# Moving diagonal, level-32 and decay-copy work off VectorE in a bidirectional HGRN2 scan, with uneven filler between half heads

## The chip, the cores and the metric

The kernel runs on one core of one Trainium2 chip. The core has a matmul engine (TensorE, PE in the profile; PEld is its weight load), VectorE (DVE), ScalarE (ACT), GpSimd (POOL) and SyncE (SP), each with its own instruction queue that runs in order. Data is moved by DMA, issued here from the SP queue and from the POOL queue. The metric is the device time of one execution in microseconds. The kernel before takes 1859.93 us, the median of three runs (1857.55 to 1863.16).

## The reference

One layer of a bidirectional encoder on x of 1 x 1024 x 1024, float32. The parts that matter here are the token mixers; the convolution module and the feed-forward net stand around them.

```
h    = rmsnorm(x)
proj = h @ w_in                  # glu, q, v, z_f, z_b, og, g_a, g_b
a    = convolution module(glu)
o    = scan(q, z_f, v) + reversed scan(q, z_b, v)      # 8 heads of 128
b    = (rmsnorm of each head of o) * norm_w * silu(og)
x    = x + (sigmoid(g_a) * a + sigmoid(g_b) * (b @ o_w)) @ w_out
x    = x + conv_glu_ffn(rmsnorm(x));   out = rmsnorm(x)

# scan, per head, for one direction:
f   = lb + (1 - lb) * sigmoid(z);   k = (1 - lb) * sigmoid(-z)
S_t = diag(f_t) S_{t-1} + k_t v_t^T;   o_t = S_t^T q_t
```

Inside a chunk of 128 positions the scan becomes a matrix of scores (each pair of positions with the product of the decays between them), and from chunk to chunk a 128 x 128 state is carried, forward for one direction and backward for the other.

## The kernel before

A matmul of the large projections is done three times (high part by high part, high by low, low by high; lines 144 to 146 in `mm3`), with each operand split by ScalarE (line 122, the high part) and VectorE (line 119, the rest). The projection runs in three stretches. A first part of `w_in` runs beside the convolution module, as pairs of column tiles by a seven-product scheme; its weight sums are accumulating DMAs from the POOL queue (line 242). The last 22 column tiles of `w_in` are kept as `dense`, a stream of small steps. One step of `dense` is six matmuls of 128 x 512. They are the filler of the head stage. After the head stage come the projections `hgrn_o_w` and `w_out`, and the feed-forward net.

The head stage (lines 1123 to 1160) goes over eight heads and, inside each, two half heads of 512 positions (four chunks of 128). Everything on PE stands in the order of the program, so the loop itself sets what PE does. On the other engines a scheduler orders the instructions ahead of time, within what the data allows, and each engine's queue then runs in that order.

For each half head there are these parts:

- `scan_inputs` loads q and the two gate inputs and makes f and the keys on ScalarE; line 872 clips f on VectorE.
- `scan_base` turns f into products of decays within blocks of 8 positions, in a buffer `DE` (lines 890 to 909, VectorE), and makes the scaled queries and keys `Qh`, `Kh`, `qF` and `kG` (lines 919 to 931). It is run one half head ahead, in small steps (`ahead.step`).
- `scan_levels` builds the scores `S_t` (128 x 4 x 128) in levels of 8, 16, 32 and 64 positions. At each level ScalarE copies the keys into `A` (line 945), PE multiplies (line 948), and the result is put into the places of `S_t` that belong to the level: at 8 by a plain copy (line 972) and two predicated copies for the blocks of 8 (line 975), at 16 and 32 by a predicated copy under a mask (line 979), at 64 by two block copies on ScalarE (line 983). VectorE then scales `kG` and `qF` for the next level. The diagonal of the second direction is kept apart in one buffer `dg` (line 977), and added to `S_t` at the end (line 995, VectorE).
- `scan_states` transposes `kG`, copies it (`kT`, line 1006) and makes the state updates (line 1013).

The outputs of a head are made while the next head runs. `outputs` first carries the backward states through (line 1106, six steps on VectorE), and then `scan_outputs` multiplies (line 1054), sums squares on ScalarE (line 1059), takes the reciprocal root on POOL (lines 408 and 409, `rstd_small`), scales on ScalarE (line 1073), transposes and gates (line 1082) and stores. Its `yield`s cut it into places.

The loop calls `between` seven times per half head: four times in the levels, three in the states. Each call issues `FILL` steps of `dense` (a fraction is carried over), two steps of the base of the next half head, and one place of the pending outputs:

```
            def between(fill):
                dense.fill(fill)
                if ahead is not None:
                    ahead.step(BASE_STEPS)
                pending.fill(1)
```

After the loop the last head's outputs are issued by hand among what is left of `dense` (lines 1162 to 1176).

Of the kernel before, what the change touches and what calls it, by code (L numbers as in the profile page):

```python
# [13 lines left out]
U8 = mybir.dt.uint8  # L14
AF = mybir.ActivationFunctionType
ALU = mybir.AluOpType
AX = mybir.AxisListType

P = 128
FILL = 1.3  # L20
CONV_FILL = 1.6
NPAIRS = 17
LN_FILL = 6
# [22 lines left out]
def tile_hybrid_encoder(  # L46
# [24 lines left out]
    V, A, G, T = nc.vector, nc.scalar, nc.gpsimd, nc.tensor  # L71
# [638 lines left out]
    m_b = cp.tile([P, P], U8, name="m_b")  # L710
    m_d = cp.tile([P, P], U8, name="m_d")
    m_16 = cp.tile([P, P], U8, name="m_16")
    m_32 = cp.tile([P, P], U8, name="m_32")

    def build_masks():
        it = mp.tile([P, P], I32, tag="tm", name=nm("it"), bufs=4)
        ip = mp.tile([P, P], I32, tag="tm", name=nm("ip"), bufs=4)
        G.iota(it, pattern=[[1, P]], base=0, channel_multiplier=0)
        G.iota(ip, pattern=[[0, P]], base=0, channel_multiplier=1)
        xo = mp.tile([P, P], I32, tag="tm", name=nm("xo"), bufs=4)  # L720
        V.tensor_tensor(xo, it, ip, op=ALU.bitwise_xor)
        fs = mp.tile([P, 4, P], F32, tag="tm", name=nm("fs"), bufs=4)
        V.tensor_copy(fs[:, 0, :], xo)
        V.tensor_tensor(fs[:, 1, :], it, ip, op=ALU.subtract)
        ge = fs[:, 1, :]
        V.tensor_scalar(m_d, fs[:, 0, :], 0.0, None, op0=ALU.is_equal)
        V.tensor_scalar(fs[:, 2, :], fs[:, 0, :], 8.0, None, op0=ALU.is_lt)
        V.tensor_scalar(fs[:, 3, :], ge, 0.0, None, op0=ALU.is_ge)
        V.tensor_tensor(m_f, fs[:, 2, :], fs[:, 3, :], op=ALU.mult)
        V.tensor_scalar(fs[:, 3, :], ge, 0.0, None, op0=ALU.is_lt)  # L730
        V.tensor_tensor(m_b, fs[:, 2, :], fs[:, 3, :], op=ALU.mult)
        for m, h in ((m_16, 16.0), (m_32, 32.0)):
            V.tensor_scalar(fs[:, 2, :], fs[:, 0, :], h, None, op0=ALU.is_ge)
            V.tensor_scalar(fs[:, 3, :], fs[:, 0, :], 2 * h, None, op0=ALU.is_lt)
            V.tensor_tensor(m, fs[:, 2, :], fs[:, 3, :], op=ALU.mult)

    build_masks()

# [109 lines left out]
    def c4(t):  # L848
        return t.rearrange("p (c t) -> p c t", c=4)
# [25 lines left out]
    def scan_base(ins):  # L875


        q, f, kk, ks = ins

        def two(t, *r):  # L880
            if len(r) == 1:
                return view(t, r[0], [[8, N2]])
            return view(t, r[0], [[r[1] - r[0], 2], [8, N2]])

        fv = lambda *r: two(f, *r)
        ed = lambda *r: two(DE, *r)
        D = D0


        V.tensor_copy(ed(2, D + 4), fv(3, 4))  # L890
        tt(ed(1, D + 5), fv(2, 4), fv(3, 5))
        yield
        tt(ed(0, D + 6), fv(1, 6), ed(1, D + 5))
        tt(ed(D + 7), ed(D + 6), fv(7))
        yield
        V.reciprocal(ed(D, 7), ed(0, D + 7))
        yield

        fm = hp.tile([P, 2, NB], F32, tag="fm", name=nm("fm"), bufs=2)
        turned = view(fm, NB, [[-NB, 2], [1, NB]])  # L900
        tt(turned, view(f, 0, [[H, 2], [8, NB]]), view(DE, E0, [[H, 2], [8, NB]]))
        tb = hp.tile([P, 3, NB], F32, tag="tb", name=nm("tb"), bufs=3)
# [12 lines left out]
        along = [[8, NB], [1, 8]]  # L915
        for d in range(2):
            m0, st = ((0, 1), (7, -1))[d]
            whole = [[8, NB], [st, 8]]
            tt(view(Qh, (1 - d) * H + m0, whole), view(q, m0, whole), view(DE, D + d * H, along))
            yield  # L920
            keys(
                view(Kh, d * H + m0, whole),
                view(kk, d * H + m0, whole),
                ks[:, d : d + 1],
                view(DE, d * H, along),
            )
            yield
        both = [[H, 2], [8, NB], [1, 8]]
        tt(view(qF, 0, both), view(Qh, 0, both), view(fm, 0, [[NB, 2], [1, NB], [0, 8]]))
        yield  # L930
        tt(view(kG, 0, both), view(Kh, 0, both), view(DE, D + 7, [[H, 2], [8, NB], [0, 8]]))
        yield
        yield qF, kG, [(Qh[:, 1 - d, :], Kh[:, d, :]) for d in range(2)], tb

    def scan_levels(base, S_t, Tt):
# [28 lines left out]
        def over(m):  # L964
            return view(m, 0, [[0, 4], [1, P]])

        for h in (8, 16, 32, 64):
# [3 lines left out]
            if h == 8:  # L971
                A.copy(S_t, b)
                for d, m in ((0, m_f), (1, m_b)):
                    bi = inside(d)
                    V.copy_predicated(S_t, over(m), bi)
                    if d == 1:
                        V.copy_predicated(c4(dg), over(m_d), bi)
            elif h < 64:
                V.copy_predicated(S_t, over(m_16 if h == 16 else m_32), b)
            else:  # L980
                for s0 in range(0, P, h):
                    t0 = s0 ^ h
                    A.copy(S_t[s0 : s0 + h, :, t0 : t0 + h], b[s0 : s0 + h, :, t0 : t0 + h])
# [8 lines left out]
            tt(to, view(tb, 0, [[nb, k], [2, n]]), view(tb, 1, [[nb, k], [2, n]]))  # L992
            tb = tn
            yield
        V.tensor_tensor(S_t, S_t, c4(dg), op=ALU.add)

    def scan_states(i, kG, v, Tt, Sf, Sb):

# [37 lines left out]
    def scan_outputs(h, kept, Sf, Sb):  # L1036
# [28 lines left out]
            if half == 0:  # L1065
                yield
        rstd_small(rs, ss, DK)
        yield
        yield
        for half in range(2):  # L1070
            for c in range(4):
                sl = slice(c * P, (c + 1) * P)
# [28 lines left out]

    def outputs(h, kept, Tt, Sf, Sb):
        for c in range(5, -1, -1):
            hf, cc = c // 4, c % 4
            n1, c1 = (c + 1) // 4, (c + 1) % 4
            V.scalar_tensor_tensor(
                Sb[hf][:, cc, :],
                Sb[n1][:, c1, :],
                Tt[:, n1, 1, c1 : c1 + 1],
                Sb[hf][:, cc, :],  # L1110
                op0=ALU.mult,
                op1=ALU.add,
            )
        yield
        yield from scan_outputs(h, kept, Sf, Sb)
# [12 lines left out]
    for h in range(NH):  # L1128
# [4 lines left out]
        for half in range(2):  # L1133
# [13 lines left out]
            for n, _ in enumerate(scan_levels(base, S_t, Tt[:, half])):  # L1147
                if n == 2:
# [2 lines left out]
                        T.transpose(b[:, c * P : (c + 1) * P], vl[:, c * P : (c + 1) * P], ident)  # L1151
                    v = hp.tile([P, 4, DK], F32, tag="v", name=nm("v"), bufs=3)
                    A.copy(v.rearrange("p c e -> p (c e)"), b)
                between(FILL)
            qF, kG = base[0], base[1]
            for _ in scan_states(i, kG, v, Tt, Sf, Sb):
                between(FILL)
            kept.append((S_t, v, qF))
            cur = ahead
        pending = Stream(outputs(h, kept, Tt, Sf, Sb))  # L1160

    left = 8 * (len(rest) - 2) + 16 - dense.count
    pending.fill(1)
    dense.fill(left - 20)
    pending.fill(1)
    dense.fill(4)
    pending.fill(2)
    dense.fill(4)
    pending.fill(2)
    dense.fill(4)  # L1170
# [323 lines left out]
```

## Time and profile before

| | us |
|---|---|
| runs, median (lowest, highest) | 1859.93 (1857.55, 1863.16) |
| profiled execution, its own time | 1873.26 |
| profiled execution, span from first to last instruction | 1871.5 |
| PE busy in the span | 1788.6 |
| VectorE busy | 1275.7 |
| ScalarE busy | 796.2 |
| POOL busy | 185.8 |

A profile shows one execution. The page gives busy time of each engine, the span in 40 slices with the busy share of each in tenths, the costliest groups of instructions, and the DMA issues. Its other views answer for a stretch of time: busy time by stretch, which waits were long and who ended them, groups of instructions with their mean duration, and the single instructions in order of time. Rows name an instruction by engine, line of the kernel, operation, and its tiles as output<-input. PE's matmuls overlap, so its busy time is not a measure of how well it is used; gaps between its rows are.

### The profile page before, as it was taken

The numbers are of one execution on the slowest core, as the hardware profiler recorded it, in microseconds if no ns is written. First come the engines' busy times: TensorE is split into PE (matmuls) and PEld (weight loads), VectorE is DVE, ScalarE is ACT, GpSimd is POOL, SyncE is SP. The second block draws the span as 40 slices with busy tenths as digits, with TensorE's granted clock in tenths as the row PEclk, the third lists the DMA queues.
The fourth block names the chain that finished last, engine by engine and source line by source line (L and its number), as shares of the span: only waits on it lengthen the run. The fifth ranks groups of instructions, "written<-read, shape, count | busy, mean of one in ns | idle before, by whom it ended". The sixth has DMA issues, their size and how long they took to land.

```text
span 1871.5 us, 23768 instructions
## 1 busy us (share of the span) xinstructions
PE 1788.6 (96%) x8574; PEld 1481.4 (79%) x8574; DVE 1275.7 (68%) x1874; ACT 796.2 (43%) x1483; POOL 185.8 (10%) x197
## 2 busy tenths in 40 slices
PE   7989999999999999999989999899999999899996
PEld 6868777777778888888878787688888888788885
DVE  4599999534479999999835565666666667534445
ACT  6443333234545566556442244443444434522124
POOL 1201111213000000000000001111111111000000
PEclk9999999999999999999999999999999999999998
DMA  7658878775653333332238665676776765633134
GB/s 268 213 141 185 184 170 198 184 170 130 208 186 96 113 113 117 98 108 91 74 110 239 191 193 190 152 156 144 150 153 149 156 146 130 208 97 95 55 86 169
DMA packets 323468, 281.42 MB, mean 150 GB/s; under 512 B 14734, under 2 KB 246934, under 8 KB 323350
## 3 DMA queue, kind: packets, MB, share of 16 engines
q1 hardware_dynamic: 272886, 240.05, 41.4%
q0 software_dynamic: 50464, 39.85, 14.9%
q8 instruction: 67, 1.10, 0.3%
q14 instruction: 51, 0.42, 0.1%
HBM read 188.09 MB, written 71.83 MB: 139 GB/s over the span
## 4 chain that ended last, share of the span: by engine, by line
PE 45%; DVE 23%; DMA 18%; ACT 6%; issue 5%; POOL 1%; SPq 0%; ACTq 0%; POOLq 0%; DVEq 0%
PE mm L144 12%; PE mm L145 12%; PE mm L146 12%; DMA wr<-wr 4%; DVE wp L119 3%; DMA wr<-sw 3%; DMA sw<-in_w_in_dram 3%; DMA tm<-d_a 3%; DVE kG L840 2%; DVE acc L755 2%; PE sc L144 2%; PE sc L146 2%; PE sc L145 2%; DVE qF L840 2%; DVE DE L840 2%
## 5 line engine op out<-in xcount | busy, mean ns | idle before, releaser
L144 PE MATMUL mm<-hx,wp 128*128 128x512 f32 x1176 | 480.1, 408 | 23.8 <-DVE ev L541 6.8
L146 PE MATMUL mm<-hx,wp 128*128 128x512 f32 x1176 | 464.9, 395 | 1.9 <-DVE wp L119 1.9
L145 PE MATMUL mm<-hx,wp 128*128 128x512 f32 x1176 | 464.6, 395 | 0.5 <-DVE hx L476 0.5
L122 ACT CAST wp<-wr 128x1024 fp32r<-128x1024 f32 (+2 forms) x193 | 176.7, 915 | 344.8 <-PE mm L145 188.3
L119 DVE TENSOR_TENSOR wp<-wr,wp 128x1024 fp32r<-128x1024 f32 (+2 forms) x193 | 203.4, 1054 | 123.0 <-ACT wp L122 116.2
L144 PEld LDWEIGHTS mm<-hx,wp 128*128 128x128 f32 x1176 | 224.7, 191 | 72.9 <-DVE ev L541 9.7
L146 PEld LDWEIGHTS mm<-hx,wp 128*128 128x128 f32 x1176 | 224.1, 191 | 52.5 <-DVE wp L119 3.7
L145 PEld LDWEIGHTS mm<-hx,wp 128*128 128x128 f32 x1176 | 224.7, 191 | 43.0 <-DVE hx L476 0.8
L755 DVE SCALAR_TENSOR_TENSOR acc<-gl,v_b,acc 128x1024 f32<-128x1024 f32 x120 | 150.0, 1284 | 0.5
L1370 DVE TENSOR_TENSOR xr<-mm,xr 128x512 f32<-128x512 f32 x48 | 33.1, 690 | 80.4 <-PE mm L146 80.4
L948 PE MATMUL sc<-qF,A 128*128 128x128 f32 x512 | 69.8, 280 | 13.3 <-DVE qF L840 13.1
L948 PEld LDWEIGHTS sc<-qF,A 128*128 128x128 f32 x512 | 65.2, 195 | 20.4 <-issue 14.9
L242 POOL DMA_DIRECT2D wr<-sw x38 | 33.8, 889 | 442.8 <-DVE wp L119 153.1
L122 ACT CAST wq<-sw 128x1024 fp32r<-128x1024 f32 x39 | 41.0, 1051 | 77.1 <-PE mm L145 59.5
L945 ACT COPY A<-kG 128x512 f32<-128x512 f32 x64 | 39.6, 618 | 73.8 <-DVE kG L840 51.3
L1292 DVE SCALAR_TENSOR_TENSOR tm<-gp,v_a,tm 128x512 f32<-128x512 f32 x88 | 65.6, 746 | 3.3 <-ACT tm L1288 2.5
L144 PE MATMUL mm<-hy,wp 128*128 128x512 f32 x156 | 62.2, 399 | 3.1 <-ACT su L270 2.9
L145 PE MATMUL mm<-hy,wp 128*128 128x512 f32 x156 | 61.9, 396 | 0.7 <-DVE hy L119 0.7
L270 ACT COPY su<-mm 128x512 f32<-128x512 f32 x78 | 45.1, 578 | 39.2 <-PE mm L146 39.2
L144 PE MATMUL tr<-hx,wp 128*128 128x512 f32 x156 | 61.4, 394 | 0.0
L146 PE MATMUL mm<-hy,wp 128*128 128x512 f32 x156 | 61.1, 392 | 0.0
L144 PE MATMUL sc<-hy,wq 128*128 128x512 f32 x156 | 61.1, 392 | 0.0
(322 smaller groups left out, 3601.5 us busy)
## 6 DMA issues: line engine op xcount, KB each, us to landing
wr<-in_w_in_dram SPq DMA_DIRECT2D x53, 512.0 KB
sw<-in_ffn_w_up_dram SPq DMA_DIRECT2D x44, 256.0 KB
sw<-in_ffn_w_up_dram POOLq DMA_DIRECT2D x22, 512.0 KB, 9.2
wr<-in_ffn_w_up_dram SPq DMA_DIRECT2D x22, 512.0 KB
d_g<-ft SPq DMA_DIRECT2D x44, 256.0 KB
ev<-d_g SPq DMA_DIRECT2D x44, 256.0 KB
wr<-sw POOLq DMA_DIRECT2D x38, 256.0 KB, 3.2
wr<-wr POOLq DMA_DIRECT2D x38, 256.0 KB, 4.8
```

Of the source, the lines that this page charges most:

```text
L119: eng.tensor_tensor(lo, src, hi.bitcast(F32), op=ALU.subtract)
L122: A.copy(hi, src)
L144: T.matmul(acc, whi[:, k, :], ahi, start=first, stop=False, skip_group_check=again)
L145: T.matmul(acc, whi[:, k, :], alo, start=False, stop=False, skip_group_check=again)
L146: T.matmul(acc, wlo[:, k, :], ahi, start=False, stop=last, skip_group_check=again)
L242: G.dma_start(o, a, accum_op=ALU.add)
L270: A.copy(t, acc)
L755: V.scalar_tensor_tensor(acc, g[:, k : k + S], tap(k), acc, op0=ALU.mult, op1=ALU.add)
L840: V.tensor_tensor(o, a, b, op=op)
L945: A.copy(A_t.rearrange("p (b x e) -> p b x e", x=2, e=h), pairs(kG, h))
L948: T.matmul(b[:, c * P : (c + 1) * P].rearrange("p (b x e) -> p b x e", x=2, e=h), A_t[:, c * P : (c + 1) * P], view(qF, c * P, [[2 * h, P ...
L1292: V.scalar_tensor_tensor(c, g[:, o + k : o + k + H], vec("fdw", k * NF + j), c, op0=ALU.mult, op1=ALU.add,)
```

## The change

Five things are changed in the head stage, and one mask is no longer built.

1. The filler: `FILL` becomes 1.1 steps for each place of the first half head and 1.5 for the second.
2. The outputs take eleven places instead of eight: the chain of backward states is cut in two, and four places instead of two lie between the reciprocal root and the scaling. The calls after the loop are changed to match.
3. The diagonal is added to `S_t` by an accumulating DMA from the POOL queue instead of an addition on VectorE.
4. Level 32 is put into `S_t` by four block copies of 32 partitions on ScalarE, as level 64 is by two, instead of a predicated copy on VectorE. The mask `m_32` goes.
5. The first strided copy of `scan_base` (line 890) is on ScalarE instead of VectorE.

```diff
-FILL = 1.3
+FILL = (1.1, 1.5)
...
-    m_32 = cp.tile([P, P], U8, name="m_32")
...
-        for m, h in ((m_16, 16.0), (m_32, 32.0)):
-            V.tensor_scalar(fs[:, 2, :], fs[:, 0, :], h, None, op0=ALU.is_ge)
-            V.tensor_scalar(fs[:, 3, :], fs[:, 0, :], 2 * h, None, op0=ALU.is_lt)
-            V.tensor_tensor(m, fs[:, 2, :], fs[:, 3, :], op=ALU.mult)
+        V.tensor_scalar(fs[:, 2, :], fs[:, 0, :], 16.0, None, op0=ALU.is_ge)
+        V.tensor_scalar(fs[:, 3, :], fs[:, 0, :], 32.0, None, op0=ALU.is_lt)
+        V.tensor_tensor(m_16, fs[:, 2, :], fs[:, 3, :], op=ALU.mult)
...
-        V.tensor_copy(ed(2, D + 4), fv(3, 4))
+        A.copy(ed(2, D + 4), fv(3, 4))
...
-            elif h < 64:
-                V.copy_predicated(S_t, over(m_16 if h == 16 else m_32), b)
+            elif h == 16:
+                V.copy_predicated(S_t, over(m_16), b)
             else:
                 for s0 in range(0, P, h):
                     t0 = s0 ^ h
...
-        V.tensor_tensor(S_t, S_t, c4(dg), op=ALU.add)
+        G.dma_start(S_t.rearrange("p c t -> p (c t)"), dg, accum_op=ALU.add)
...
         rstd_small(rs, ss, DK)
-        yield
-        yield
+        for _ in range(4):
+            yield
...
     def outputs(h, kept, Tt, Sf, Sb):
         for c in range(5, -1, -1):
+            if c == 2:
+                yield
...
-                between(FILL)
+                between(FILL[half])
...
-    pending.fill(1)
+    pending.fill(2)
     dense.fill(left - 20)
     pending.fill(1)
     dense.fill(4)
-    pending.fill(2)
+    pending.fill(4)
```

More of the change, by code (lines that the diff above doesn't have):

```diff
@@ L1153, in tile_hybrid_encoder @@
                     A.copy(v.rearrange("p c e -> p (c e)"), b)
-                between(FILL)
+                between(FILL[half])
             qF, kG = base[0], base[1]
             for _ in scan_states(i, kG, v, Tt, Sf, Sb):
-                between(FILL)
+                between(FILL[half])
             kept.append((S_t, v, qF))
```

## The prediction

> **What bounds the kernel now.** I read the page first for the whole span, then busy time by stage, then the waits of the head stage, then its timeline. The stage in question is the loop over heads, from about 555 to 946 us.
>
> ```profile
> span 1871.5 us, 23768 instructions
> PE 1788.6 (96%) x8574; PEld 1481.4 (79%) x8574; DVE 1275.7 (68%) x1874; ACT 796.2 (43%) x1483; POOL 185.8 (10%) x197
> PE   7989999999999999999989999899999999899996
> DVE  4599999534479999999835565666666667534445
> ...
> 555.00:946.00 391.00, 370.95 (x2359) 327.27 (x2360) 359.37 (x666) 212.80 (x489) 13.79 (x14) 0.99 0.32 100
> 617.21:639.08 21.87, 18.70 (x119) 16.11 (x118) 17.72 (x35) 10.57 (x23) 1.33 (x1) 1.00 0.37 121
> 639.08:668.95 29.87, 29.74 (x195) 26.58 (x194) 29.80 (x57) 18.91 (x46) 0.61 (x2) 1.00 0.33 98
> ```
>
> The last three rows are busy time by stretch: length, then PE, PEld, DVE, ACT, POOL, clock, DMA share. Over the head stage PE is busy 370.95 of 391 us, so 20.05 us of PE idle time is all that any edit here can win, unless PE work goes away, and none does. DVE is busy 359.37 us, 92%; by the tenths DVE is at 9 only here and in the convolution stage. The last two rows are one half 1 and the following half 0, cut at the diagonal additions that end each. They are unequal. In half 0 (29.87 us) both PE and DVE are full. In half 1 (21.87 us) PE idles 3.17 us and DVE 4.15 us. Half 0 carries the previous head's outputs on top of the same seven shares of filler.
>
> What ends PE's idle time, by the waits of 560 to 935 us (waiter, releaser, total, times, longest), and two of these in the timeline:
>
> ```profile
> PE sc L948 <- DVE qF L840: 9.6, 9, 1.9
> PE sc L1013 <- ACT kT L1006: 5.6, 7, 1.3
> PE sc L961 <- ACT Sb L1031: 1.7, 2, 1.5
> ACT tm L1073 <- POOL ors L409: 9.2, 7, 1.6
> DVE kG L840 <- ACT A L945: 7.0, 4, 2.7
> ...
> 723.20 1.16 PE L1013 MATMUL sc<-v,kT 128*128 128x128 f32 x8 [0.77 <-ACT kT L1006]
> 736.31 1.13 PE L948 MATMUL sc<-qF,A 128*128 128x128 f32 x8 [1.94 <-DVE qF L840]
> ```
>
> More than half of PE's named waits are for DVE's qF update, the rest for ScalarE's kT and Sb copies. ScalarE in turn stands 9.2 us in seven heads waiting for POOL's rstd before it can scale the outputs (L1073), with kT and A copies queued behind; so an output step that comes too soon also costs.
>
> **The change part by part.** First the three operations taken from VectorE, and what stands for them on ScalarE (mean ns, 560 to 935 us):
>
> ```profile
> L979 DVE COPY_PREDICATED S<-m,sc 128x512 f32<-128x512 uint8 x28 | 20.4, 727 | 0.0
> L995 DVE TENSOR_TENSOR S<-S,dg 128x512 f32<-128x512 f32 x15 | 10.0, 668 | 0.2
> L890 DVE COPY DE<-f 128x256 f32<-128x256 f32 x14 | 6.0, 432 | 0.0
> ...
> L865 ACT ACTIVATE f<-zi,lbw 128x512 f32<-128x512 f32 x26 | 21.2, 815 | 0.1
> L983 ACT COPY S<-sc 64x256 f32<-64x256 f32 x30 | 10.9, 365 | 12.9 <-PE sc L948 9.6 <-DVE Kh L843 3.0
> L1033 ACT COPY Sb<-sc 128x128 f32<-128x128 f32 x7 | 1.9, 273 | 0.0
> ```
>
> VectorE loses, per half head, one of the two predicated copies (0.727), the diagonal addition (0.668) and the strided copy (0.432): 1.83 us, and 16 x 1.83 = 29.2 us over the stage. That is more than PE's 20.05 us of idle time, so PE must become the limit.
>
> ScalarE gains four copies of 32 partitions by 128 elements and one strided copy of 256 elements per half head. Its 128-element copy takes 0.273 and its 256-element one 0.365; I take 0.273 each (same elements per partition), 1.09 us, with 0.365 as the upper end, 1.46. The strided copy lies between 0.365 (256 elements, rows of 64) and 0.815 (512 elements with scale and bias); I take 0.45, near VectorE's own 0.432. That is 1.54 us per half head (1.46 to 2.28), 25 us over the stage. ScalarE goes from 212.8 to 238 us of some 377: 63%. As busy time it is covered; its cost can only be order, since ScalarE works in order and the new copies stand between A and kT copies that PE and VectorE wait for. Two couplings are new. VectorE's third DE product now waits for ScalarE's strided copy (in the built order it carries such a wait); two or more VectorE operations stand between, the f clip and a kG update among them, so I cost it at nothing, with 16 x 2.7 = 43 us as the upper end, from the longest wait of kG for an A copy above. And the level-32 copies let their bank go by ScalarE instead of VectorE, which no longer holds it behind its backlog: nothing, or a small gain.
>
> The diagonal goes to POOL's queue as an accumulating transfer of 256 KB inside SBUF. The weight sums use the same form and size (L242: durations of the issue on POOL; page 6: median us to landing):
>
> ```profile
> L242 POOL DMA_DIRECT2D wr<-sw x38: 865/887/932, 135.0 to 1574.5; - x38
> ...
> wr<-sw POOLq DMA_DIRECT2D x38, 256.0 KB, 3.2
> wr<-wr POOLq DMA_DIRECT2D x38, 256.0 KB, 4.8
> ...
> 614.81 0.37 ACT L983 COPY S<-sc 64x256 f32<-64x256 f32 x1
> 628.90 0.72 DVE L977 COPY_PREDICATED dg<-m_d,ob 128x512 f32<-128x512 uint8 x1
> 637.87 0.75 ACT L983 COPY S<-sc 64x256 f32<-64x256 f32 x2 [0.29 <-PE sc L948]
> 651.58 0.72 DVE L977 COPY_PREDICATED dg<-m_d,ob 128x512 f32<-128x512 uint8 x1
> 616.61 0.20 POOL L408 TENSOR_SCALAR ors<-oss 128x8 f32<-128x8 f32 x1 [97.01 <-ACT jk L1059]
> ```
>
> It can start when the last level-64 copy is done (615.18, 638.62) and the next write of the single dg buffer waits for it (628.90, 651.58): 13.7 and 13.0 us of room against 0.89 + 4.8 = 5.7. The matmuls that read S come later still. POOL is busy 13.79 us in the stage and takes 14 us more. The rstd pair of a head now stands in POOL's order behind the transfer of half 0, which is released at 615.18, before rstd's own 616.61; and the scaling that waits for rstd moves three places later. So I cost it at nothing.
>
> A rule speaks against this. The Trainium skill, page "SBUF — State Buffer", section on the two sides of the memory, says that VectorE and GpSimd share a port pair under an exclusive lock, so that descriptor writing and VectorE's two-port modes block each other whole. No row of this stage can show it, POOL issuing nothing there. It is priced below as a rival.
>
> Next, filler and outputs. The count of one fill step is six matmuls:
>
> ```profile
> 563.49 0.39 PE L146 MATMUL mm<-hx,wp 128*128 128x512 f32 x1
> 564.85 0.39 PE L146 MATMUL mm<-hx,wp 128*128 128x512 f32 x1
> ...
> 708.63 0.39 PE L1054 MATMUL ob<-Sb,qF 128*128 128x128 f32 x2
> 713.08 1.22 DVE L840 TENSOR_TENSOR qF<-Qh,fm 128x1024 f32<-128x1024 f32 x1
> ...
> L733 DVE TENSOR_SCALAR fs<-fs x2: 211/214/216, 133.2 to 136.0; 128x128 f32<-128x128 f32 x2
> ```
>
> Six matmuls from start to start are 564.85 - 563.49 = 1.36 us. Each half has seven places: half 0 goes from 9.1 to 7.7 steps and half 1 from 9.1 to 10.5, so 1.4 x 1.36 = 1.9 us of PE work moves from the full half into the one with 3.17 us of idle time. The total stays 18.2 per head, and what remains after the loop too. The outputs' eight places become eleven of fourteen: the Sb chain takes two, both output products go one place later, and scaling, transposes and stores of d_bm go four later, into half 1. On the SP queue those stores now stand behind the next loads instead of ahead, where their buffers allow it. The order also brings the first output product nearer to the qF write that reuses its buffer: it ends at 709.0 and the write starts at 713.08, 4.1 us of room. One place later costs a level, a v transpose and a fill step, about 3.0 us, which leaves 1.1; nothing, or 1 us of VectorE's relief in each of 7 heads. The places in the tail are filled to match (two, one, four, two, one), so nothing changes there. Three VectorE operations of the mask (0.2 us each) go, in the convolution stage: under 1 us.
>
> **The sum.** In half 0 PE's demand falls by 1.9 us, and VectorE's by 1.83, from the same 29.8 us: both come to 28.0. In half 1 PE takes 18.70 + 1.9 = 20.6 of 21.87 and VectorE 17.72 - 1.83 = 15.9, so both still fit. So a head saves about 1.85 us; with seven such half 0s and a little from the first head, 7.5 x 1.85 = 13.9 us, 14 us. PE's idle time of the stage would go from 20 to 6 us. All stages after are unchanged and hand it through. The profiled execution took 1873.26 us (span 1871.5), 13 us or 0.7% over the median of 1859.93; I take the difference over to the median: 1859.9 - 14 = 1846 us, range of this case 1840 (all 20 us gone) to 1853.
>
> **The rivals.**
> - The port lock: VectorE is held during each descriptor write. 16 x 0.887 = 14.2 us of VectorE's 29.2 come back and half of the gain goes: 14 - 7 = 7, so 1853. This is what the page named above would give at worst. For it: 16 clips and the products with two SBUF inputs run all the time. Against: VectorE then still has 15 us less than before.
> - ScalarE's round trips stay. Of the PE waits above, 7.3 us are for kT and Sb, and less filler in half 0 covers them less. If these double and only the qF part goes, 9.6 - 7.3 = 2 us remain: 1858, no measurable difference.
> - Slower: VectorE's DE product waits for the strided copy, which on ScalarE stands behind a kT copy that waits for PE. Its price is 16 times the lateness; it decides from 29.2 / 16 = 1.83 us, where it eats the relief. At the 2.7 us of the longest wait above: 16 x (2.7 - 1.83) = 14 us, 1874. For it: ScalarE does stand before such copies (kG for A, 7.0 us in four). Against: only four times in sixteen, and the outputs' bunch on ScalarE is thinned.
> - The transfer does not land in 13 us: each us over it costs up to 15. Its 5.7 us speak against it.
>
> **How the numbers follow.** Forecast 0.60, port lock 0.10, round trips 0.13, ScalarE's copy 0.14, late transfer 0.03. About 0.3%, 5.6 us, is what a measurement of this kernel can tell from no change. Faster holds the first two, 0.70; same 0.13; slower 0.17. The range reaches from 1838 (all idle time and 2 us of the convolution stage) to 1864, which takes in the round trips and the small end of ScalarE's copy and leaves out its 1874.
>
> **What would show it.** In the profile after, the head stage is some 14 us shorter and VectorE's busy share in it falls to about 87%; halves come nearer to 28 and 22 us; PE's idle time in it is near 6 us; the waits for qF and for ors are gone or small; POOL shows 16 issues of some 0.89 us with dg never a releaser. Wrong if DE on VectorE has waits on ScalarE, dg waits on a DMA, or kT and Sb waits of PE grow.

## The result, and the profile after

The changed kernel takes 1876.47 us (median of 5 runs, 1873.88 to 1879.20); the kernel before took 1861.05 us beside it (5 runs, 1857.55 to 1864.15). The ratio is 1.0082, 95% interval 1.0064 to 1.0101: 0.8% slower, some 15 us. The forecast was 1846 us, faster.

The work went where the change put it. The page of the kernel after, its span and its busy time by engine:

```profile
span 1874.7 us, 23882 instructions
PE 1786.6 (95%) x8574; PEld 1480.4 (79%) x8574; DVE 1254.3 (67%) x1823; ACT 818.4 (44%) x1563; POOL 200.1 (11%) x213
DVE  4599999534479888889735555666666667534445
```

DVE is 21.4 us less busy than before, ACT 22.2 and POOL 14.3 us more; in the head stage's slices DVE fell from 9 to 8 tenths. For the stage I use one cut for all kernels from here on: from the first to the last `v` copy of the sixteen half heads. Busy time by stretch of before, then of after (length, PE, PEld, DVE, ACT, POOL, clock, DMA share):

```profile
559.89:941.44 381.55, 364.27 (x2327) 321.44 (x2327) 351.89 (x653) 210.86 (x486) 13.79 (x14) 0.99 0.32 101
```

```profile
556.13:944.57 388.44, 364.88 (x2313) 321.85 (x2312) 334.12 (x611) 230.04 (x557) 26.75 (x29) 0.99 0.36 106
```

VectorE has 17.8 us less to do in the stage, and the stage is 6.9 us longer. PE does the same work; its idle time (length less PE) rose from 17.28 to 23.56 us. Which waits, from those of after in this stretch (waiter, releaser, total, times, longest):

```profile
DVE f L870 <- ACT f L863: 11.3, 7, 3.2
PE sc L946 <- DVE qF L838: 10.9, 12, 2.0
ACT tm L1071 <- POOL ors L409: 9.8, 7, 2.1
DVE kG L838 <- ACT A L943: 9.2, 7, 2.3
PE sc L959 <- ACT Sb L1029: 8.7, 5, 2.2
DVE DE L838 <- ACT DE L888: 5.8, 6, 1.2
PE sc L1011 <- ACT kT L1004: 1.4, 2, 1.2
```

Against before, PE's wait for qF is not shorter (9.6 there), that for kT fell from 5.6 to 1.4, and that for the Sb copy rose from 1.7 to 8.7 us. ScalarE still waits for `ors` in all seven heads. And VectorE, with 17.8 us less to do, idles almost 25 us more (54.3 against 29.7): its wait for `f` from ScalarE rose from 4.3 to 11.3 us, that for the keys in `A` from 7.0 to 9.2, and the one for ScalarE's strided copy (`DE`), 5.8 us, is new. The timeline of after, around one start of half 1, shows how the Sb wait comes about:

```profile
666.01 0.58 ACT L1004 COPY kT<-tr 128x512 f32<-128x512 f32 x1
668.38 1.83 POOL L409 TENSOR_TENSOR ors<-ors,mhalf 128x8 f32<-128x8 f32 x1
670.25 0.69 ACT L1071 ACTIVATE tm<-tm,ors 128x128 f32<-128x128 f32 x2 [1.96 <-POOL ors L409]
672.27 1.85 ACT L1071 ACTIVATE tm<-tm,ors 128x128 f32<-128x128 f32 x6
674.03 0.46 ACT L1029 COPY Sb<-sc 128x384 f32<-128x384 f32 x1
674.53 1.16 PE L959 MATMUL sc<-Qh,Kh 128*128 128x128 f32 x8 [1.85 <-ACT Sb L1029]
```

ScalarE waits 1.96 us for the root, does the scaling (L1071; a weight cast and the copy of a filler bank stand between its two groups), and only then copies Sb, which empties the bank that PE's next product (L959) needs. In the kernel before four of the eight scalings stood between the two kT copies instead (the same view, the same head):

```profile
667.29 0.59 ACT L1006 COPY kT<-tr 128x512 f32<-128x512 f32 x1
670.25 1.28 ACT L1073 ACTIVATE tm<-tm,ors 128x128 f32<-128x128 f32 x4 [1.37 <-POOL ors L409]
671.44 0.56 ACT L1006 COPY kT<-tr 128x512 f32<-128x512 f32 x1
```

By one mark the halves became more even. ScalarE's last block copy of level 64 marks the end of the scores of a half head; of before (the first and last of seven heads, end of half 1) and of after (the same two, and between them one half 0 and one half 1):

```profile
586.33 0.75 ACT L983 COPY S<-sc 64x256 f32<-64x256 f32 x2 [3.06 <-PE sc L948]
944.71 0.75 ACT L983 COPY S<-sc 64x256 f32<-64x256 f32 x2 [2.69 <-PE sc L948]
```

```profile
579.99 0.75 ACT L981 COPY S<-sc 64x256 f32<-64x256 f32 x2 [0.94 <-PE sc L946]
607.37 0.37 ACT L981 COPY S<-sc 64x256 f32<-64x256 f32 x1
632.18 0.74 ACT L981 COPY S<-sc 64x256 f32<-64x256 f32 x2 [2.85 <-PE sc L946]
946.64 0.74 ACT L981 COPY S<-sc 64x256 f32<-64x256 f32 x2
```

Over the seven heads half 0 takes 28.2 us on average before and 26.9 after, half 1 takes 23.0 and 25.5. Half 0 gave 1.3 us, half 1 took 2.5. (358.38 and 366.65 us in all.) That is where ScalarE stands, not PE; PE's own halves are shown under "The order taken apart".

The two profiles place 6.9 us of the loss. The rest of the 15 us can't be read from them, because before's profiled execution is itself 12 us above the median of its runs (its granted clock, 0.984, is the lowest that any execution of that kernel shows; others have up to 0.993). So the experiments are judged by the ratio of their medians, and the stage is used for which wait moved.

### The profile page after: what moved, and what is told of

Its sections match the earlier page's. It is cut to its first block, busy times and chain, and to the rows that moved or that the text cites. A ratio compares the mean times of both kernels' runs of the same rounds, so it can differ in the third digit from the quotient of the medians.

```text
span 1874.7 us, 23882 instructions
## 1 busy us (share of the span) xinstructions
PE 1786.6 (95%) x8574; PEld 1480.4 (79%) x8574; DVE 1254.3 (67%) x1823; ACT 818.4 (44%) x1563; POOL 200.1 (11%) x213
## 4 chain that ended last, share of the span: by engine, by line
PE 40%; DMA 6%; DVE 4%; ACT 2%; issue 1%; POOL 0%; ACTq 0%; POOLq 0%; SPq 0%; DVEq 0%
PE mm L144 10%; PE mm L145 10%; PE mm L146 10%; DMA tm<-d_a 3%; PE sc L144 2%; PE sc L146 2%; PE sc L145 2%; DMA sw<-in_ffn_w_up_dram 1%; PE tr L145 1%; PE tr L146 1%; PE tr L144 1%; DMA ev<-d_g 1%; DMA wr<-wr 1%; PE ob L1052 1%; DVE tm L1189 1%
## 5 line engine op out<-in xcount | busy, mean ns | idle before, releaser
L144 PE MATMUL tr<-hx,wp 128*128 128x512 f32 x156 | 61.2, 392 | 0.0
L144 PE MATMUL sc<-hy,wq 128*128 128x512 f32 x156 | 61.1, 392 | 0.0
L146 PE MATMUL sc<-hy,wq 128*128 128x512 f32 x156 | 61.0, 391 | 0.0
L146 PE MATMUL tr<-hx,wp 128*128 128x512 f32 x156 | 60.7, 389 | 0.0
```

Of the source, the lines that this page charges most:

```text
L144: T.matmul(acc, whi[:, k, :], ahi, start=first, stop=False, skip_group_check=again)
L146: T.matmul(acc, wlo[:, k, :], ahi, start=False, stop=last, skip_group_check=again)
```

## The experiments

All ratios are to the kernel before, run beside each. The waits are PE's, in the head stage; idle is the length less PE's busy time; a dash says that the view lists no such wait. The kT column holds the row `sc <- kT` alone: with the product in the other bank (`ob <- kT`) PE waited 3.8 us more for kT in e5_strided, 1.6 in e7_no_adds, 1.1 in e8_qf_first, 1.0 in e2_engines, and 0.6 or less elsewhere.

| run | ratio (95% interval) | stage us | PE idle | qF | kT | Sb |
|---|---|---|---|---|---|---|
| before | 1 | 381.55 | 17.28 | 9.6 | 5.6 | 1.7 |
| after | 1.0082 (1.0064, 1.0101) | 388.44 | 23.56 | 10.9 | 1.4 | 8.7 |
| e1_order | 1.0064 (1.0038, 1.0091) | 389.00 | 24.23 | 11.9 | 0.6 | 9.5 |
| e2_engines | 1.0054 (1.0033, 1.0076) | 388.00 | 22.16 | 10.4 | 5.8 | 2.0 |
| e3_diag | 1.0019 (0.9999, 1.0038) | 381.10 | 16.08 | 8.6 | 6.8 | - |
| e4_scalar | 1.0058 (1.0036, 1.0079) | 387.45 | 22.40 | 7.7 | 8.0 | 1.9 |
| e5_strided | 1.0101 (1.0082, 1.0119) | 396.20 | 26.29 | 7.0 | 5.5 | 2.5 |
| e6_level32 | 1.0043 (1.0027, 1.0059) | 383.80 | 19.42 | 6.7 | 11.5 | 0.3 |
| e7_no_adds | 0.9998 (0.9984, 1.0013) | 376.60 | 15.36 | 5.8 | 6.9 | - |
| e8_qf_first | 1.0009 (0.9994, 1.0024) | 384.50 | 16.96 | 3.5 | 8.6 | 1.8 |
| e9_places | 1.0024 (1.0008, 1.0041) | 386.71 | 19.84 | 11.3 | 0.5 | 7.2 |
| e10_fill | 0.9998 (0.9983, 1.0013) | 381.08 | 18.10 | 5.4 | 11.2 | 1.0 |
| e11_spare | 1.0031 (1.0013, 1.0048) | 387.46 | 20.63 | 8.3 | 10.0 | 1.7 |
| e12_gap6 | 0.9961 (0.9941, 0.9980) | 372.32 | 10.46 | 6.4 | 3.2 | 0.8 |
| e13_gap4 | 1.0006 (0.9982, 1.0030) | 378.33 | 14.37 | 4.1 | 6.2 | 1.6 |
| e14_cut_gap5 | 1.0005 (0.9984, 1.0026) | 384.23 | 19.34 | 10.4 | 0.9 | 6.5 |
| e15_gap6_diag | 0.9967 (0.9948, 0.9986) | 369.64 | 9.78 | 5.1 | 3.3 | - |
| e16_gap6_full | 0.9993 (0.9971, 1.0015) | 374.60 | 12.35 | 6.1 | - | 3.0 |
| e17_gap8 | 0.9968 (0.9950, 0.9986) | 372.08 | 10.66 | 6.0 | 3.3 | 1.0 |
| e18_gap6_qfirst | 0.9932 (0.9912, 0.9952) | 368.42 | 7.00 | 2.9 | 2.7 | 1.0 |

**The order or the engines?** e1_order is before with parts 1 and 2 of the change (uneven filler, eleven places), e2_engines is before with parts 3 to 5 (diagonal, level 32, strided copy).

> The uneven filler and the eleven places alone; diagonal, level 32 and strided copy stay on VectorE. Theory A (the order costs: the scaling of the outputs now stands on ScalarE at the start of half 1, ahead of the Sb copy that the second product of level 8 waits for): this alone is slower by 8 to 16 us than before, and PE's waits for Sb are as long as in the changed kernel (8.7 us against 1.7 before). Theory B (the work moved to ScalarE costs): within 4 us of before or faster by some us, because filler moved into the half with idle time. Theory C (the DMA costs): as B.

> Diagonal by DMA, level 32 and strided copy on ScalarE; filler 1.3 and eight places as before. Theory A: faster than before by 5 to 15 us, as VectorE is relieved of 29 us. Theories B and C: slower by 8 to 16 us, with VectorE's waits for ScalarE longer than before.

Both are slower than before, so neither half of the change is a gain spoiled by the other. Only e1_order has the Sb waits (9.5 us) of the changed kernel. The loss of e2_engines, 7.7 us, is just under the 8 expected. The two losses, 0.64 and 0.54%, add to more than the 0.82% of both together, but by no more than the intervals allow; whether they share idle time is open.

**The three moves one at a time.** e3_diag, e4_scalar (4 and 5 together), e5_strided, e6_level32:

```diff
-        V.tensor_tensor(S_t, S_t, c4(dg), op=ALU.add)                      # e3
+        G.dma_start(S_t.rearrange("p c t -> p (c t)"), dg, accum_op=ALU.add)
-        V.tensor_copy(ed(2, D + 4), fv(3, 4))                              # e4, e5
+        A.copy(ed(2, D + 4), fv(3, 4))
-            elif h < 64:                                                   # e4, e6
+            elif h == 16:
```

> Only the diagonal moves, to the accumulating DMA. Theory C: slower by 8 us or more, VectorE waiting for the DMA before it writes dg, or its clip and its products lengthened beside the descriptor writes. Theories A and B: faster by 2 to 8 us, as VectorE loses 10.7 us of 359 in the head stage and nothing waits.

> Only level 32 and the strided copy move, to ScalarE. Theory B: slower by 8 us or more; the strided copy, 0.7 us on ScalarE against 0.43 on VectorE, keeps VectorE's third DE product waiting, and the four copies delay kT, Sb and A copies. Theories A and C: faster by 3 to 10 us, as VectorE loses 18.5 us.

> Only the strided copy moves to ScalarE. If it is the costly one of the two of the run before (0.7 us on ScalarE in place of 0.43, in front of A and kT copies): slower by 5 us or more. If the four level-32 copies are: within 3 us.

> Only level 32 moves to ScalarE, the mask of 32 goes. If the four copies are the costly ones (about 1.05 us per half head in ScalarE's order, between the A copies): slower by 5 us or more, with PE waiting longer for kT and A copies. If the strided copy is: within 3 us or faster.

The transfer can't be told from no change; the 2 to 8 us that two of the theories gave it did not come. The loss of e2_engines is that of the two moves to ScalarE. In e6_level32 PE's kT wait doubles, 5.6 to 11.5 us. The strided copy alone is the worst kernel of all, though less is on ScalarE than in e4_scalar; so it isn't busy time that costs but what happens to stand ahead of what. One such place, from its timeline:

```profile
931.85 1.23 DVE L840 TENSOR_TENSOR qF<-Qh,fm 128x1024 f32<-128x1024 f32 x1
932.33 3.32 POOL L408 TENSOR_SCALAR ors<-oss 128x8 f32<-128x8 f32 x1 [46.69 <-ACT jk L1059]
932.99 0.69 DVE L840 TENSOR_TENSOR qF<-qF,tb 128x512 f32<-128x512 f32 x1
933.59 0.69 DVE L995 TENSOR_TENSOR S<-S,dg 128x512 f32<-128x512 f32 x1
934.19 1.23 DVE L840 TENSOR_TENSOR kG<-Kh,DE 128x1024 f32<-128x1024 f32 x1
937.40 0.40 ACT L1073 ACTIVATE tm<-tm,ors 128x128 f32<-128x128 f32 x1 [5.16 <-POOL ors L409]
937.82 0.58 ACT L1006 COPY kT<-tr 128x512 f32<-128x512 f32 x1
938.46 1.16 PE L1013 MATMUL ob<-v,kT 128*128 128x128 f32 x8 [1.75 <-ACT kT L1006]
```

POOL's first step of the root, 0.20 us in most heads, takes 3.32; ScalarE stands 5.16 us before the scaling, the kT copy behind it, and PE behind that. It happens once at this length in that execution. Of the stage's 14.65 us over before, 9.0 are PE's idle time, in the main waits for A (5.7 us, none before) and for kT (9.3 us with both products, 5.6 before); 5.6 are busy time of PE. Why this order is so much worse than e4_scalar's stays open.

**Is VectorE the bound?** e7_no_adds leaves out the level-32 write into `S_t` and the diagonal addition, and gives them to nobody (its output is not the reference's):

> Level 32 is not put into the scores at all and the diagonal is not added (its output is therefore not the reference's); the mask of 32 is not built. VectorE loses 22 us and no engine gains work. If VectorE's load bounds the head stage, as the prediction had it: faster by 8 to 15 us. If the order of the engines' round trips bounds it, and not VectorE's load: within 4 us of before, VectorE's busy share falling to about 87%, PE's idle time in the stage staying above 14 us.

No change, 0.9998, though VectorE's busy time in the stage fell by 13.7 us, to 338.23. The qF waits of that profile fell by 3.8 us and those for kT rose by 2.9 (both products), and the runs are no faster. In this order VectorE's load is not what the time goes by.

**One round trip eased.** e8_qf_first issues VectorE's qF update ahead of the writes of the scores:

```diff
             tt(pairs(kG, h), pairs(kG, h), view(tb, 1, [[2, n], [nb - 1, 2], [0, h]]))
+            tt(pairs(qF, h), pairs(qF, h), view(tb, nb + 1, [[2, n], [nb - 1, 2], [0, h]]))
...
-            tt(pairs(qF, h), pairs(qF, h), view(tb, nb + 1, [[2, n], [nb - 1, 2], [0, h]]))
```

> The kernel before, with the update of qF issued ahead of the writes into the scores at each level, so that VectorE does it earlier; no work is added or taken away. If PE's waits for qF (13 us in the stage) come from the place of that update in VectorE's order: they fall below 6 us and the kernel is faster by 3 to 8 us. If they come from VectorE's load: no change beyond 3 us.

The 13 us of the expectation are the wait for qF over the whole span; in the stage it was 9.6. The waits of e8_qf_first:

```profile
PE sc L1013 <- ACT kT L1006: 8.6, 7, 3.2
PE sc L948 <- DVE qF L840: 3.5, 3, 1.7
```

The qF wait fell by 6 us and the kT wait took 3 to 4 of it: nothing gained (1.0009).

**The order taken apart.** e9_places is part 2 alone, e10_fill part 1 alone:

> The kernel before with the eleven places of the outputs alone (the Sb chain cut in two, four places instead of two ahead of the scaling, the calls after the loop to match); the filler stays at 1.3 for each place, VectorE and ScalarE keep their work. If the loss of the order (1.0064 for uneven filler and eleven places together) comes from where the scaling stands on ScalarE: PE's waits for the Sb copy at about 9 us as there, those for kT near 1.5 us, ratio 1.004 to 1.008. If it comes from the uneven filler: waits for Sb near 2 us and a ratio within 0.3 % of 1. By the prediction (the outputs' bunch on ScalarE is thinned): qF and ors waits gone, faster by 5 to 14 us.

> The kernel before with the uneven filler alone (1.1 steps for each place of the first half head, 1.5 for the second), the outputs in eight places. By the prediction: 1.9 us of PE work for each head goes from the full half into the idle time of the other, faster by up to 14 us, 0.993. If round trips bound and the filler between is what covers them: half 0, where the outputs already cover, loses little and half 1 gains little, ratio 0.998 to 1.002, PE idle of the stage near the 17 us of before. If the uneven filler is what costs in the order: 1.004 to 1.008.

The filler is neutral. It trades qF waits (9.6 to 5.4) for kT waits (5.6 to 11.2): in the stage, of before and of e10_fill alike, every wait for kT stands in half 0, which loses filler, and all but one of those for qF in half 1, which gains it. The eleven places cost 0.24%, less than the 0.4% or more that the theory gave, and bring the Sb waits.

What each half gained or lost has to be read on PE itself. PE runs in program order, so its first product inside the blocks of 8 (`sc<-Qh,Kh`) cuts the halves where the program does. The means of the profiled executions from one such row to the next, over half 0 of the last seven heads and half 1 of heads two to seven:

| us | half 0 | PE busy | idle | half 1 | PE busy | idle |
|---|---|---|---|---|---|---|
| before | 27.8 | 26.7 | 1.1 | 23.6 | 22.2 | 1.4 |
| e10_fill | 26.7 | 24.9 | 1.8 | 24.7 | 23.9 | 0.8 |
| e9_places | 28.0 | 26.3 | 1.7 | 24.1 | 22.9 | 1.1 |
| after | 27.3 | 24.5 | 2.8 | 25.5 | 25.0 | 0.5 |

In e10_fill the 1.9 us of filler did move, but half 0 became only 1.1 us shorter, since PE waits longer for kT in it, and half 1 became as much longer. In the changed kernel half 0 has 2.2 us less of PE's work and is 0.5 us shorter: PE idles 2.8 us in it, of which the waits for Sb, which all stand at its end, are 1.2 (8.7 us in seven heads). By ScalarE's copies of level 64 e9_places has two equal halves, 25.9 and 25.9; PE's halves moved there by 0.5 us at most. The filler and the eleven places together cost 0.64% (e1_order); the intervals of e1_order and e9_places overlap, so whether the filler makes the places worse is open.

**ScalarE's time by itself.** e11_spare adds the level-32 copies and lets VectorE keep its own:

```diff
                 V.copy_predicated(S_t, over(m_16 if h == 16 else m_32), b)
+                if h == 32:
+                    spare = hp.tile([P, 4, 32], F32, tag="spare", name=nm("spare"), bufs=2)
+                    for s0 in range(0, P, h):
+                        t0 = s0 ^ h
+                        A.copy(spare[s0 : s0 + h, :, :], b[s0 : s0 + h, :, t0 : t0 + h])
```

> The kernel before with the four 32-partition level-32 copies on ScalarE done in addition, into a spare tile; VectorE keeps its predicated copy, so ScalarE takes 16 x 4 x 0.256 = 16.4 us more and VectorE nothing less. If what costs is ScalarE's time ahead of its A and kT copies: slower by at least as much as with the copies moved (1.0043), kT and A waits of PE above 8 us. If the cost there came from the order that the move gave to VectorE or from the bank being held by ScalarE: at or below 1.002.

Slower by 0.31%, with kT waits of 10 us. e6_level32 with VectorE relieved is 0.43% slower (the intervals overlap): no gain from the relief shows, and the copies on ScalarE cost about the same with it and without.

**Where the scaling stands.** e12_gap6 leaves the chain of backward states in one place and puts six places, not two, ahead of the scaling; e13_gap4 has four; e14_cut_gap5 has the chain cut in two and five, so that its scaling is issued at the places nine and ten, as in e12_gap6. (The changed kernel: cut, four, places eight and nine.)

```diff
         rstd_small(rs, ss, DK)
-        yield
-        yield
+        for _ in range(6):         # e13: 4; e14: 5, with the chain cut
+            yield
...
-    pending.fill(2)
+    pending.fill(6)
```

> The kernel before with six places between the reciprocal root and the scaling (two before, four in the changed kernel), so that the scaling is issued at the places nine and ten of fourteen, away from the first products of half 1; filler 1.3 everywhere, Sb chain in one place. If a scaling next to a copy that PE waits for is what costs, and its place alone decides: both waits small (kT under 3 us, Sb under 3 us), stage shorter by 3 to 6 us, ratio 0.996 to 0.999. If the round trips simply hand the wait on to the next one, as with the qF update issued first: the sum of PE's waits stays at 15 to 18 us and the ratio within 0.3 % of 1.

> The kernel before with four places instead of two between the reciprocal root and the scaling, the Sb chain in one place: the step in the placing of the outputs that the changed kernel shares with the faster kernel of six places. With the cut of the chain it gave 1.0024 and Sb waits of 7.2 us. If the cut costs (it makes both output products, the squares and the root one place later, so that ScalarE meets the root's wait in half 1's start): 0.996 to 0.999, Sb waits under 3 us. If the place of the scaling costs: 1.001 to 1.004, Sb waits of 5 us or more.

> The kernel before with the chain cut in two and five places ahead of the scaling, so that the scaling is at places nine and ten as in the faster kernel of six places, one place later than in the changed kernel; filler 1.3. If the cut costs: 1.001 to 1.004 as with the eleven places, Sb waits near 7 us. If the place of the scaling alone decides: 0.995 to 0.998, PE's named waits near 10 us as there.

e12_gap6 is faster than before. With the scaling at the same places, the cut costs 0.44% (0.9961 against 1.0005, intervals apart), and the two kernels with the cut and the even filler show Sb waits of 6.5 and 7.2 us; of those that change only places and filler, none without the cut has over 1.7. Without the cut, two places later for the scaling gain 0.45% (1.0006 to 0.9961, intervals just apart) and halve the kT waits; the first two places later, from before to e13_gap4, gained nothing (1.0006). How the cut works can be seen in the timelines around a start of half 1, first of e9_places (cut):

```profile
669.76 0.58 ACT L1006 COPY kT<-tr 128x512 f32<-128x512 f32 x1
671.54 0.43 POOL L408 TENSOR_SCALAR ors<-oss 128x8 f32<-128x8 f32 x1 [49.83 <-ACT jk L1059]
673.72 1.28 ACT L1073 ACTIVATE tm<-tm,ors 128x128 f32<-128x128 f32 x4 [0.84 <-POOL ors L409]
675.41 1.27 ACT L1073 ACTIVATE tm<-tm,ors 128x128 f32<-128x128 f32 x4
676.59 0.46 ACT L1031 COPY Sb<-sc 128x384 f32<-128x384 f32 x1
677.10 1.16 PE L961 MATMUL sc<-Qh,Kh 128*128 128x128 f32 x8 [1.93 <-ACT Sb L1031]
```

and of e12_gap6 (no cut):

```profile
660.41 0.20 POOL L408 TENSOR_SCALAR ors<-oss 128x8 f32<-128x8 f32 x1 [46.96 <-ACT jk L1059]
661.45 0.57 ACT L1006 COPY kT<-tr 128x512 f32<-128x512 f32 x1
662.41 0.70 ACT L1073 ACTIVATE tm<-tm,ors 128x128 f32<-128x128 f32 x2 [0.39 <-POOL ors L409]
664.95 1.86 ACT L1073 ACTIVATE tm<-tm,ors 128x128 f32<-128x128 f32 x6
666.71 0.46 ACT L1031 COPY Sb<-sc 128x384 f32<-128x384 f32 x1
667.23 1.16 PE L961 MATMUL sc<-Qh,Kh 128*128 128x128 f32 x8 [0.57 <-ACT Sb L1031]
```

With the cut the output products, their squares and so the root come one place later: POOL starts it 1.8 us after the second kT copy instead of 1.0 before it, and the scaling falls on the seam of the halves, where PE needs kT, Sb and A from ScalarE within a few us. A program place is not a place in ScalarE's queue, though: in e12_gap6 the scheduler still sets six scalings ahead of Sb, and what seems to help is that they are ready earlier against it (0.57 us of wait instead of 1.93). The cut also moves the output products and splits the chain on VectorE; no run separates these from the later root.

**The moves again, in the better order.** e15_gap6_diag is e12_gap6 with the transfer; e16_gap6_full is the changed kernel without the cut and with six places; e17_gap8 is e12_gap6 with eight places; e18_gap6_qfirst is e12_gap6 with the qF update first.

> The kernel before with six places ahead of the scaling and the diagonal by the accumulating transfer; VectorE loses 16 x 0.668 = 10.7 us and ScalarE takes nothing. If with the round trips eased VectorE's qF update is the wait that is left (6.4 us there): 2 to 5 us faster than with six places alone, 0.993 to 0.995. If VectorE's load is no bound here either, as in the run that left work out: 0.995 to 0.997, the same as six places alone.

> The changed kernel with the chain of backward states in one place and six places ahead of the scaling: the uneven filler and all three moves off VectorE are in it. If the loss of 0.8 % was the cut and the place of the scaling alone: 0.992 to 0.996. If ScalarE's 5 added copies per half head cost by themselves what they cost in the old order (1.0054): 1.000 to 1.003, about 0.5 % above six places alone, with waits for kT, Sb and A above 8 us together.

> The kernel before with eight places ahead of the scaling, which is then issued at the places eleven and twelve of fourteen, in the levels of half 1 and two places further from its first products than with six. If what gains is that the scaling leaves the round trips at the seam of the halves: the same as six places or better, 0.993 to 0.997. If the scaling only has to find another place, and in the levels stands ahead of A copies: A waits appear, 0.998 to 1.002.

> The kernel before with six places ahead of the scaling and the qF update issued ahead of the write of the scores. Alone, the qF update first handed its wait to kT (qF 9.6 to 3.5 us, kT 5.7 to 8.6) and gained nothing, 1.0009. If with kT and Sb eased nothing stands behind to take the wait: qF waits fall from 6.4 us to under 3, others stay under 5 us, 0.992 to 0.995. If a chain of round trips sets the pace whatever its first link: the sum of named waits stays near 10 us and the ratio at 0.995 to 0.998.

The busy time of the stage of e16_gap6_full, then of e18_gap6_qfirst with two of its waits:

```profile
559.84:934.44 374.60, 362.25 (x2313) 319.99 (x2312) 332.76 (x611) 231.64 (x557) 26.79 (x29) 1.00 0.38 110
```

```profile
555.80:924.22 368.42, 361.42 (x2319) 320.42 (x2319) 349.74 (x652) 209.65 (x485) 14.26 (x14) 1.00 0.32 101
PE sc L948 <- DVE qF L840: 2.9, 5, 1.1
PE sc L1013 <- ACT kT L1006: 2.7, 3, 1.9
```

With all its other parts kept, the changed kernel is level with before once the chain is whole and the scaling comes later: 0.9993 against 1.0082. So the cut and the four places instead of six cost the changed kernel 0.9%. That is not the whole account of its 0.8%, for six places gain 0.4% over before too: beside them the moves and the filler still seem to cost some 0.3% (0.9993 against 0.9961; the intervals overlap, so this is not settled), and in the old order the moves cost 0.54% alone. The changed kernel with the eight places of before, which would part the two shares, was not run. The transfer again does nothing in either sense. Eight places do as well as six. With the qF update first as well, e18_gap6_qfirst is the best kernel here: 0.9932, 1852.03 us (median of 6 runs) against 1863.24, about 11 us faster than before. Its qF waits fell from 6.4 to 2.9 us and no other wait took them over. What the qF update itself adds to the six places is not settled, since the intervals of 0.9961 and 0.9932 overlap.

## Why the prediction was wrong

- **PE's idle time of 20 us is all there is to win**: right. The best kernel takes PE's idle time from 17.28 to 7.00 us and the stage from 381.55 to 368.42 us (by two single executions); PE's busy time, 360 to 370 us over the runs, moves by some us besides, its granted clock between 0.99 and 1.00.
- **"PE must become the limit", since VectorE loses more than PE idles**: this is the step that failed. It took a busy share of 92% for a bound. VectorE's relief was there (17.8 us by busy time; my 29.2 added durations that overlap in the records), but leaving out 22 us of VectorE's operations (13.7 by busy time) left the time at 0.9998, and half 0 on PE at 27.8 us. PE waits for one qF update at a time, for when it comes and not for how much VectorE has to do: issuing it earlier cut that wait by 6 us, leaving work out by 3.8, relieving VectorE in the changed kernel not at all, and neither of the first two alone made the kernel faster. What the change did add, it added to waits: for Sb by the later outputs (e1_order, 0.64% with the filler) and through ScalarE's new copies (e4_scalar, 0.58%). Both were put at nothing in the sum.
- **Half 0 is full and half 1 has room**: the sum of the halves failed with it, by where they were cut. VectorE's diagonal addition comes late against PE's order in half 0, so the two stretches are not two half heads: they hold 42 and 67 filler products (lines 144 to 146), where the program gives each half 54.6. Cut on PE itself, the halves idle 1.1 and 1.4 us. There were not 3.17 us of room for the 1.9 us of filler, and half 0 did not end 1.9 us sooner when they left it: it ended 1.1 us sooner in e10_fill and 0.5 in the changed kernel, the rest being mainly waits for kT and Sb. Evenness was no aim either: the fast kernel has 26.8 and 22.8 us by the same cut.
- **"The outputs' bunch on ScalarE is thinned"**, the scaling three places later (one passage of the prediction says four; counted in the program it goes from places five and six to eight and nine): wrong in sign. The move in program order put it from between the kT copies to ahead of the Sb copy, at the seam. The waits for `ors` stayed (9.2 to 9.8 us). I counted the places between root and scaling, not those ahead of the root: with the scaling at the same places nine and ten these waits are 4.6 us without the cut and 9.9 with it. Four places do not do it even without the cut (9.9 in e13_gap4).
- **ScalarE's added copies cost nothing but order**: the mechanism was named, its price of nothing was wrong. The 32-partition copies took 0.256 us (0.273 taken), the strided copy 0.698 (0.45 taken, from a bound of 0.815). In the old order they cost 0.58% together. The rival that I set against this, DE waiting for the strided copy (1874 us, close to the 1876.47 measured), is not the cause, and its nearness in number is luck: that wait is 5.8 us in six, longest 1.2, under the 1.83 us from which it was to decide, and the order alone is slower without it.
- **ScalarE's round trips stay**: the rival that was nearest in mechanism. I let them cancel the gain; they grew from 7.3 us (kT and Sb) to 10.1, and no qF part came off. Its reason, less filler in half 0, holds for kT in e10_fill; in the changed kernel the Sb waits come with the cut.
- **The transfer costs nothing**: right. Of the stage after, the groups of instructions:

```profile
L981 ACT COPY S<-sc 32x128 f32<-32x128 f32 x64 | 16.4, 256 | 30.2 <-PE sc L946 27.8 <-DVE DE L838 1.8
L993 POOL DMA_DIRECT2D S<-dg x15 | 13.3, 888 | 347.9 <-ACT S L981 197.9 <-DVE qF L838 59.6 <-DVE tb L838 27.4
L888 ACT COPY DE<-f 128x256 f32<-128x256 f32 x14 | 9.8, 698 | 0.0
L870 DVE TENSOR_SCALAR f<-f 128x1024 f32<-128x1024 f32 x13 | 9.0, 691 | 11.4 <-ACT f L863 11.3
```

Issues of 0.888 us, as taken, a landing after 4.4 us (4.8 taken), and nothing waits for the transfer. VectorE's clip takes 691 ns against 683 before, but in this profile no clip ran beside an issue, so that alone does not decide the port lock. In e3_diag some did, this one from end to end:

```profile
766.28 0.96 POOL L995 DMA_DIRECT2D S<-dg  x1 [25.78 <-ACT S L983]
766.44 0.68 DVE L872 TENSOR_SCALAR f<-f 128x1024 f32<-128x1024 f32 x1
```

The clip took its usual time within the issue (which took 0.96 us; those of after take 0.85 to 0.93), and in the profile after a qF update wholly within one took 0.67 us, where 0.68 is the mean before. So the rival that VectorE is held during each issue falls. The buffer of qF held up next to nothing: VectorE's waits for an output product are 0.5 us in all, once.

## What to carry to other kernels

A high busy share says how much an engine does, not that the others wait for its load: ask of each wait which single instruction ends it, and what stands ahead of that in its queue. On an in-order engine that serves short round trips, a batch of deferred work (here eight scalings behind a reduction) is best released where no such copy is due; moving it "later" by places also moves what it depends on, so count from the reduction, and read the built queue. A wait eased alone can hand its time to the next, as the qF update did to kT (1.0009); the later scaling, which eased kT and Sb, did gain (0.9961). And cut a stretch on the engine whose work you add up: marks of another engine, which may run behind, put the work of one half into the other.

## What the runs showed of the hardware

- The strided copy of 256 elements by 128 partitions takes VectorE 432 ns and ScalarE 698, nearly twice the 362 to 365 ns of its block copies of 64 partitions by 256 elements from a bank to `S_t`. Which of the strides, the partitions or the source costs this was not tried.
- In e5_strided a POOL instruction of 128 x 8 elements took 3.32 us instead of 0.20 while four VectorE operations with two inputs in SBUF (three products and the diagonal addition) ran one behind the other, and ended 0.23 us after the last of them (934.19 + 1.23 = 935.42, and 932.33 + 3.32 = 935.65). Two more in that run took 1.78 and 0.92 us and ended 0.06 us after such a series. The Trainium skill, page "SBUF — State Buffer", section "SBUF: two separate sides", gives a port pair of VectorE and GpSimd under an exclusive lock and counts VectorE operations with two SBUF inputs among its holders, against a GpSimd operation that reads SBUF, as this one does. The row agrees; it also shows POOL held through several operations, not one. If that lock is the cause, which no run tested, it bit POOL and not VectorE, and through the in-order scaling PE.
- Two executions of one kernel differ by more than the parts of this change: before's runs beside the experiments span 1856.34 to 1874.74 us, so a single profile's stage is a witness for which wait moved, not for 0.3%. A part of the spread goes with the granted clock: of these 123 executions the 18 with 0.986 or less have a median of 1867.4 us, the 56 with 0.990 or more 1861.4.
